# Dt's sixteen fp32 products bound behind the first sum of squares in a hybrid streaming encoder layer

## The chip, the cores and the metric

The kernel runs on one core of a Trainium2 chip (trn2). The metric is device time in microseconds (us). Before the change three runs gave 1318.94, 1319.08 and 1319.94 us, so the median is 1319.08 us. Besides these there is one profiled execution, from which all rows come. The engines are named as the profile names them: PE (matmuls), PEld (PE's weight loads), DVE, ACT, POOL, and SP, which issues most DMAs.

## The reference, cut to what matters

One inference step of one layer for 256 prompt rows and 32 sample rows (NT = 288 together), model width 2048:

```
xn   = rmsnorm(x, norm_mix_pre)
proj = xn @ w_in                   # [u_pool 1024 | z 2048 | xBC 2560 | dt 32]
pool = trailing means of u_pool, projected
ssd  = chunked scan: conv and silu of xBC; dt = softplus(dt_raw + bias); gate silu(z); grouped rmsnorm
x    = x + rmsnorm(concat[pool, ssd] @ w_out)
x    = x + rmsnorm(ConvFFN(rmsnorm(x)))      # w_up 2048 -> 11264, conv, silu gate, w_down
```

The change concerns the 32 columns of dt alone. All of the layer's other work is computed by the same instructions before and after.

## The kernel before, in words

Activations lie transposed, channels on 128 partitions and the 288 rows along the free axis. Each of the large products is done in three matmuls (`mm3`, lines 135 to 137): weights and activations are split into a high part in fp32r and a low rest, and hi·hi, hi·lo and lo·hi are summed in PSUM. The split of a weight tile is one ACT instruction (`whi`, line 129; line 283 in the first projection) and one DVE instruction (`wlo`, line 130; line 284). Four buffers each hold `raw` (the weights as loaded), `whi` and `wlo`. The rows after this call the three matmuls of a step *main matmuls*; a weight tile of 1024 columns feeds 24 of them.

The instructions are written in program order, and a scheduler puts them into a fixed order for each engine when the kernel is built. Every engine then runs its own list strictly in order. `tc.issue_after(ins)` binds what is written under it behind an instruction, `tc.keep_in_program_order` fixes a matmul's place on PE, and `tc.high_priority` draws an instruction forward.

The first projection (written out at lines 255 to 295) treats six 128-column blocks of xBC: the four of B and C and the first two of x. Its loop over k (16 tiles of 128 input channels) loads `xT` and `raw`, makes `xn` (line 98 on ACT and 99 on DVE), splits the weights, and issues 18 main matmuls per k into six PSUM sums `first` (five `acc`, one `acc_x`). Meanwhile ACT squares the input tiles and POOL adds them into `xsum` (line 233). At k = 14, ahead of that tile's 18 main matmuls, `input_rstd` multiplies `xsum` by a matrix of 1/2048 (`prs`, line 241, one fp32 matmul, recorded as two), ACT takes the root (line 236) and DVE the reciprocal (line 237): that is `rstd`.

Dt has too few columns for that scheme. Its weights (`wdt`, 128 x 16 x 32) are scaled by norm_mix_pre on DVE (line 299), and 16 fp32 products of 32 columns each (`pdt`, line 304, recorded as 32) go into four quarters of one PSUM tile, so that four partial sums stand on the partitions. DVE multiplies them by `rstd` (`v4`, line 306, `v` in the profile's rows), and one more fp32 matmul with `sel4` (`pv`, line 308) adds the four quarters. From `pv` comes dt's chain on 32 partitions: softplus by a series (`ser`), the running sum `r`, the table `g` (lines 401 to 405), which SP stores to DRAM (`g_d`, line 407) and loads again spread over all partitions (`gb`, line 453, 0.8 MB for each group of four heads).

`ssd_four` uses `gb`: ACT makes `ce`, `elast` and the decay mask `m` from it (lines 460 to 474), DVE multiplies `m` by the products of B and C (line 476), and PE multiplies it with the scaled x (`py`, lines 483 to 489). Eight such groups are spread over the projections of x and z. PSUM has five `acc` banks and three banks of a second pool, which `acc_x`, `prs`, `pdt`, `pv`, `py` and the like share in turn. Sums of the first projection leave PSUM through DVE (`conv_in`, lines 341 and 342, into `ebuf`), multiplied by `rstd`.

`xT` and `wdt` lie in a memory pool that is closed behind `pv`; the mixer's tiles take its place (`aneg`, line 391, `scan_one`, line 321, `h0t`, line 455), so their first writers wait for the end of `pdt`.

## Time and profile before

| what | value |
| --- | --- |
| runs, median | 1319.08 us (1318.94 to 1319.94) |
| the profiled execution's own time | 1318.3 us |
| its span, first to last instruction | 1316.4 us |
| granted PE clock | 1.000 |
| PE busy | 1310.2 us of the span |
| DVE, ACT, POOL busy | 895.7, 671.6, 229.7 us |
| first projection with prs and pdt on PE | 5.07 to 46 us |
| projections of x and z with the scan | 46 to about 282 us |

A row of the timeline gives the start in us, the duration in us, the engine, the line, the operation with output and inputs, sizes and a count; square brackets show idle time ahead of it and what ended it. Matmuls overlap in the records (a row of 0.29 us starts 0.13 us behind the one ahead), so the cost of a matmul is the distance between starts. A row of the windows gives, for a stretch of the span, how long each engine was busy in it. A row of the waits gives an engine and line, what it waited for, the total in us, how often, and the longest.

### The profile page before, as it was taken

What the parts mean: (1) busy time and instruction counts of PE and PEld (TensorE: products, weight loads), DVE (VectorE), ACT (ScalarE), POOL (GpSimd) and SP (SyncE); (2) the same over time, 40 slices, a digit from 0 to 9 for tenths busy, and PEclk for the clock granted to TensorE, in tenths of its full rate; (3) what the DMA queues carried; (4) which work ended last, traced back from release to release, by engine and by line L of the source; (5) the groups of instructions that cost most, each with busy time, mean ns of one, the idle gap of its engine ahead of it and who ended that gap; (6) DMA issues with size and microseconds to landing.
All of it is one profiled execution on the core that took longest, in us unless ns stands there. A gap on an engine that the chain in (4) does not pass through costs nothing.

```text
span 1316.4 us, 25204 instructions
## 1 busy us (share of the span) xinstructions
PE 1310.2 (100%) x10067; PEld 1298.4 (99%) x10067; DVE 895.7 (68%) x1486; ACT 671.6 (51%) x1010; POOL 229.7 (17%) x363
## 2 busy tenths in 40 slices
PE   9999999999999999999999999999999999999998
PEld 9999999999999999999999999999999999999997
DVE  8889988679654599977766744336666666664544
ACT  7558866446543466554444433334444454444443
POOL 6321221211430200211211200001111111101110
PEclk9999999999999999999999999999999999999999
DMA  9668874465665556666444445445445554466663
GB/s 350 186 209 279 278 223 145 165 221 204 208 219 181 183 167 213 187 184 203 168 161 165 160 168 173 158 171 185 168 161 165 180 169 161 163 235 187 203 179 109
DMA packets 104996, 249.81 MB, mean 190 GB/s; under 512 B 64272, under 2 KB 70352, under 8 KB 82608
## 3 DMA queue, kind: packets, MB, share of 16 engines
q1 hardware_dynamic: 102784, 243.44, 56.3%
q0 software_dynamic: 1664, 4.59, 1.2%
q8 instruction: 78, 1.28, 0.4%
q14 instruction: 38, 0.31, 0.1%
q10 hardware_dynamic: 432, 0.19, 0.1%
HBM read 236.23 MB, written 11.95 MB: 189 GB/s over the span
## 4 chain that ended last, share of the span: by engine, by line
PE 100%; ACT 0%; issue 0%; POOL 0%; DVE 0%; POOLq 0%
PE acc L135 31%; PE acc L137 31%; PE acc L136 31%; PE acc_x L137 1%; PE acc_x L135 1%; PE acc_x L136 1%; PE py L483 1%; PE pst L780 0%; PE run_a L1121 0%; PE low L1119 0%; PE idle L249 0%; PE run_b L1134 0%; PE py L485 0%; PE pdt L304 0%; PE py L489 0%; PE py L487 0%
## 5 line engine op out<-in xcount | busy, mean ns | idle before, releaser
L130 DVE TENSOR_TENSOR wlo<-raw,whi 128x1024 fp32r<-128x1024 f32 (+1 forms) x386 | 463.4, 1202 | 321.1 <-ACT whi L129 318.5
L129 ACT ACTIVATE whi<-raw 128x1024 fp32r<-128x1024 f32 (+1 forms) x386 | 400.1, 1037 | 476.8 <-PE acc L136 375.1
L135 PE MATMUL acc<-hn,whi 128*128 128x288 f32 x1360 | 393.3, 294 | 0.0
L136 PE MATMUL acc<-hn,whi 128*128 128x288 f32 x1360 | 392.7, 293 | 0.0
L137 PE MATMUL acc<-hn,wlo 128*128 128x288 f32 x1360 | 391.9, 293 | 0.0
L135 PEld LDWEIGHTS acc<-hn,whi 128*128 128x128 f32 x1360 | 253.3, 188 | 0.4 <-ACT hn L880 0.4
L136 PEld LDWEIGHTS acc<-hn,whi 128*128 128x128 f32 x1360 | 253.4, 188 | 0.1
L137 PEld LDWEIGHTS acc<-hn,wlo 128*128 128x128 f32 x1360 | 253.3, 188 | 0.0
L135 PE MATMUL acc<-xn,whi 128*128 128x288 f32 x688 | 203.2, 296 | 0.0
L136 PE MATMUL acc<-xn,whi 128*128 128x288 f32 x688 | 201.0, 293 | 0.0
L137 PE MATMUL acc<-xn,wlo 128*128 128x288 f32 x688 | 199.6, 295 | 0.0
L135 PE MATMUL acc<-fa,whi 128*128 128x288 f32 x660 | 194.0, 294 | 0.0
L136 PE MATMUL acc<-fa,whi 128*128 128x288 f32 x660 | 193.4, 293 | 0.0
L137 PE MATMUL acc<-fa,wlo 128*128 128x288 f32 x660 | 193.1, 293 | 0.0
L135 PEld LDWEIGHTS acc<-xn,whi 128*128 128x128 f32 x688 | 129.4, 188 | 1.3 <-issue 0.9
L136 PEld LDWEIGHTS acc<-xn,whi 128*128 128x128 f32 x688 | 129.2, 188 | 0.4
L137 PEld LDWEIGHTS acc<-xn,wlo 128*128 128x128 f32 x688 | 128.1, 188 | 0.0
L135 PEld LDWEIGHTS acc<-fa,whi 128*128 128x128 f32 x660 | 124.1, 188 | 0.0
L136 PEld LDWEIGHTS acc<-fa,whi 128*128 128x128 f32 x660 | 123.9, 188 | 0.0
L137 PEld LDWEIGHTS acc<-fa,wlo 128*128 128x128 f32 x660 | 123.9, 188 | 0.0
L932 POOL COPY fc_stage<-ebuf 128x4 f32<-128x4 f32 x88 | 28.4, 323 | 523.3 <-DVE ebuf L931 523.3
L928 POOL COPY ebuf<-pf 128x2 f32<-128x2 f32 x88 | 72.4, 824 | 122.2 <-DVE fc L938 70.2
(307 smaller groups left out, 1741.9 us busy)
## 6 DMA issues: line engine op xcount, KB each, us to landing
raw<-in_w_up SPq DMA_DIRECT2D x80, 1024.0 KB, 4.8
raw<-in_w_in SPq DMA_DIRECT2D x38, 1024.0 KB, 5.2
raw<-in_w_down SPq DMA_DIRECT2D x32, 1024.0 KB, 4.8
raw<-in_w_out SPq DMA_DIRECT2D x23, 1024.0 KB, 4.8
raw<-in_w_down SPq DMA_DIRECT2D x16, 768.0 KB, 4.2
raw<-in_w_up SPq DMA_DIRECT2D x8, 896.0 KB, 4.6
gb<-g_d SPq DMA_DIRECT2D x8, 832.0 KB, 6.6
raw<-in_w_first SPq DMA_DIRECT2D x5, 768.0 KB, 7.3
```

What stands on the lines that cost most here:

```text
L129: act.activation(hi, raw[:, k : k + n, :], AF.Copy)
L130: dve.tensor_tensor(lo, raw[:, k : k + n, :], hi.bitcast(F32), op=ALU.subtract)
L135: pe.matmul(out, wh, a[:, 0, :], start=start, stop=False)
L136: pe.matmul(out, wh, a[:, 1, :], start=False, stop=False)
L137: pe.matmul(out, wl, a[:, 0, :], start=False, stop=stop)
L483: pe.matmul(y[:, 0:256], xw[:, 0, c], m[:, j, 0:256], start=True, stop=False)
L928: pool.tensor_copy(e[:, 258:260], pf[:, 4:6, i])
L932: pool.tensor_copy(fc_stage[:, :, :, i], e[:, 256:324].rearrange("p (s c) -> p s c", c=34)[:, :, 0:2])
```

## The change

Three things are written at other places; no instruction is added or taken away.

- The sum that makes `sel4` from the identity is written ahead of the first projection.
- The scaling of `wdt` on DVE is bound behind the split of the thirteenth weight tile (k = 12).
- The 16 products `pdt` are written directly behind `input_rstd()` at k = 14 and kept in program order, so ahead of the 36 main matmuls of k = 14 and 15. Their PSUM tile is requested ahead of the loop.

```diff
     first = [acc_ps.tile([P, NT], F32, tag="acc", name="acc") if m < 5 else aux([P, NT], "acc_x") for m in range(6)]
     chunks = ((0, 1), (1, 1)) + tuple((k, 2) for k in range(2, KD, 2))
+    sel4 = const.tile([P, HEADS], F32, name="sel4")
+    dve.tensor_reduce(sel4, ident.rearrange("p (q h) -> p h q", h=HEADS), axis=AX.X, op=ALU.add)
+    p_dt = aux([P, NT], "pdt")
...
             cut.append((w_hi, w_lo))
+            if k == 12:
+                with tc.issue_after(w_lo.ins):
+                    dve.tensor_tensor(
+                        wdt, wdt, g_mix_pre.unsqueeze(2).broadcast_to([P, KD, HEADS]), op=ALU.mult
+                    )
...
             if k == 14:
                 input_rstd()
+                for r in range(4):
+                    for q in range(4):
+                        i = 4 * q + r
+                        o = p_dt[HEADS * q : HEADS * (q + 1), :]
+                        tc.keep_in_program_order(
+                            pe.matmul(o, wdt[:, i, :], xT[:, i, :], start=r == 0, stop=r == 3)
+                        )
             for m in range(6):
                 c = slice(m * P, (m + 1) * P)
                 mm3(first[m], hi[:, c], lo[:, c], a, k == 0, k == KD - 1)
 
-    sel4 = const.tile([P, HEADS], F32, name="sel4")
-    dve.tensor_reduce(sel4, ident.rearrange("p (q h) -> p h q", h=HEADS), axis=AX.X, op=ALU.add)
-    dve.tensor_tensor(wdt, wdt, g_mix_pre.unsqueeze(2).broadcast_to([P, KD, HEADS]), op=ALU.mult)
-    p_ = aux([P, NT], "pdt")
-    for r in range(4):
-        for q in range(4):
-            k = 4 * q + r
-            pe.matmul(p_[HEADS * q : HEADS * (q + 1), :], wdt[:, k, :], xT[:, k, :], start=r == 0, stop=r == 3)
     v4 = const.tile([P, NT], F32, tag="spread", bufs=3, name="v4")
-    dve.tensor_tensor(v4, p_, rstd, op=ALU.mult)
+    dve.tensor_tensor(v4, p_dt, rstd, op=ALU.mult)
     first_dt = aux([HEADS, NT], "pv")
     pe.matmul(first_dt, sel4, v4, start=True, stop=True)
```

Since a scheduler makes the order, the move goes further than these lines. Three places show it; the rows are those of the built programs. In the changed kernel line numbers behind the edit are larger by eight.

On PE, at k = 14 of the first projection, the piece of the difference is this (lines that are only renumbered left aside):

```order
 L137 MATMUL acc_x<-xn,wlo 128x288
 L241 MATMUL prs<-xsum,mean 128x288
+L306 MATMUL pdt<-xT,wdt 32x288 x16
 L135 MATMUL acc<-xn,whi 128x288
 L136 MATMUL acc<-xn,whi 128x288
```

The 16 products now stand between `prs` and the first main matmul of k = 14. Where they stood before, behind the last main matmul of k = 15, the changed kernel has `pv`:

```order
L135 MATMUL acc_x<-xn,whi 128x288
L136 MATMUL acc_x<-xn,whi 128x288
L137 MATMUL acc_x<-xn,wlo 128x288
L316 MATMUL pv<-v_658,sel_151 32x288
L135 MATMUL acc<-xn,whi 128x288
```

Before, 30 main matmuls of the second projection stood between `pdt` and `pv`. Up to here both kernels now have run the same work on PE, in another order.

On DVE, around the reciprocal that makes `rstd` (`ebuf_111` to `ebuf_117` take the first four sums out of PSUM, `v_658` is v4), before:

```order
L130 TENSOR_TENSOR wlo<-raw,whi 128x1024 x2
L237 RECIPROCAL rstd<-rstd 128x288
L130 TENSOR_TENSOR wlo<-raw,whi 128x1024
L341 TENSOR_TENSOR ebuf_111<-acc,rstd 128x256
L341 TENSOR_TENSOR ebuf_113<-acc,rstd 128x256
L342 TENSOR_TENSOR ebuf_111<-acc,rstd 128x32
L341 TENSOR_TENSOR ebuf_115<-acc,rstd 128x256
L342 TENSOR_TENSOR ebuf_113<-acc,rstd 128x32
L341 TENSOR_TENSOR ebuf_117<-acc,rstd 128x256
L342 TENSOR_TENSOR ebuf_115<-acc,rstd 128x32
L342 TENSOR_TENSOR ebuf_117<-acc,rstd 128x32
L130 TENSOR_TENSOR wlo<-raw,whi 128x1024
```

and in the changed kernel:

```order
L130 TENSOR_TENSOR wlo<-raw,whi 128x1024 x2
L237 RECIPROCAL rstd<-rstd 128x288
L314 TENSOR_TENSOR v_658<-pdt,rstd 128x288
L349 TENSOR_TENSOR ebuf_111<-acc,rstd 128x256
L350 TENSOR_TENSOR ebuf_111<-acc,rstd 128x32
L349 TENSOR_TENSOR ebuf_113<-acc,rstd 128x256
L350 TENSOR_TENSOR ebuf_113<-acc,rstd 128x32
L130 TENSOR_TENSOR wlo<-raw,whi 128x1024
```

v4 comes directly behind the reciprocal, where it was behind two weight splits and eight evictions; the third weight split of the second projection comes behind two evicted sums. Further on, dt's chain on DVE stands one weight split further ahead: the last part of `g` behind the 17th split of the w_in weights, not the 18th, and the first product of `m` behind the 22nd, not the 23rd. The first `py` on PE has 815 main matmuls ahead of it, not 833.

On SP's DMA queue, where `g` goes out and comes back, before:

```order
L174 DMA xs_d<-blocks 32x9x32 x4
L457 DMA xw<-xs_d 128x2x256
L458 DMA xw<-xs_d 128x256
L114 DMA raw<-in_w_in 128x2048
L174 DMA xs_d<-blocks 32x9x32 x4
L114 DMA raw<-in_w_in 128x2048
L407 DMA g_d<-g 32x416
L174 DMA xs_d<-blocks 32x9x32 x4
L453 DMA gb<-g_d 128x1664 x2
```

and in the changed kernel:

```order
L174 DMA xs_d<-blocks 32x9x32 x4
L415 DMA g_d<-g 32x416
L465 DMA xw<-xs_d 128x2x256
L466 DMA xw<-xs_d 128x256
L461 DMA gb<-g_d 128x1664
L114 DMA raw<-in_w_in 128x2048
L174 DMA xs_d<-blocks 32x9x32 x4
L461 DMA gb<-g_d 128x1664
```

The store of `g` has moved ahead of two weight loads and one store of x, and the first load of `gb` ahead of two of each; the second `gb` stands behind one weight load and one store. Behind the point that lies at 225 us in the trace of before, all engines have the same rows with the same waits in both kernels.

## The prediction

> **What bounds the kernel now.** I read the page first: the span, each engine's busy time and the chain that ended last.

> ```profile
> span 1316.4 us, 25204 instructions
> PE 1310.2 (100%) x10067; PEld 1298.4 (99%) x10067; DVE 895.7 (68%) x1486; ACT 671.6 (51%) x1010; POOL 229.7 (17%) x363
> PE 100%; ACT 0%; issue 0%; POOL 0%; DVE 0%; POOLq 0%
> ```

> PE is busy throughout, and the chain runs over PE alone. A busy PE can still be a slow one, so I looked at the stretch in which the two orders differ, 51 to 290 us, in the windows, and then at PE's waits and PE's weight loads' waits over the whole span.

> ```profile
> 51.00:290.00 239.00, 239.00 (x1940) 233.74 (x1939) 207.74 (x386) 150.41 (x272) 53.73 (x62) 1.00 0.67 213
> ```
> ```profile
> PE idle L249 <- POOL mean L182: 1.2, 1, 1.2
> PE y_ps L1164 <- ACT diag L1163: 0.6, 1, 0.6
> ```
> ```profile
> PEld py L483 <- issue: 0.8, 5, 0.2
> PEld py L483 <- PE acc L136: 0.7, 4, 0.2
> ```

> PE is busy for all 239.00 us at a granted clock of 1.00. It waits by name twice: at the very start and near the end, neither of them in a stretch that changes. The largest waits of its weight loads at the changed places are 0.8 and 0.7 us in all. So the time of this kernel is the sum of PE's matmuls, and a change of order is worth only what it saves in passages from one kind of matmul to another, or costs in a wait that isn't there now. What a main matmul costs, and what the fp32 groups cost, shows in the timeline of PE:

> ```profile
> 36.19 0.29 PE L135 MATMUL acc<-xn,whi 128*128 128x288 f32 x1
> ...
> 38.41 0.29 PE L137 MATMUL acc_x<-xn,wlo 128*128 128x288 f32 x1
> 38.55 0.65 PE L241 MATMUL prs<-xsum,mean 128*128 128x288 f32 x2
> 38.81 0.51 PE L135 MATMUL acc<-xn,whi 128*128 128x288 f32 x1
> 39.16 0.29 PE L136 MATMUL acc<-xn,whi 128*128 128x288 f32 x1
> ...
> 43.63 0.29 PE L137 MATMUL acc_x<-xn,wlo 128*128 128x288 f32 x1
> 43.85 2.15 PE L304 MATMUL pdt<-xT,wdt 128*32 128x288 f32 x32
> 45.93 0.40 PE L135 MATMUL acc<-xn,whi 128*128 128x288 f32 x1
> 46.17 0.29 PE L136 MATMUL acc<-xn,whi 128*128 128x288 f32 x1
> ...
> 49.85 0.29 PE L137 MATMUL acc<-xn,wlo 128*128 128x288 f32 x1
> 50.07 0.67 PE L308 MATMUL pv<-v,sel 128*32 128x288 f32 x2
> 50.67 0.40 PE L135 MATMUL acc<-xn,whi 128*128 128x288 f32 x1
> 50.91 0.29 PE L136 MATMUL acc<-xn,whi 128*128 128x288 f32 x1
> ```

> From 36.19 to 38.55 there are 18 main matmuls, so one costs 0.131 us. A group's whole cost is the distance from the main matmul ahead of it to the second behind it, less two of these (0.26): `prs` 39.16 - 38.41 - 0.26 = 0.49 us, `pdt` 46.17 - 43.63 - 0.26 = 2.28, `pv` 50.91 - 49.85 - 0.26 = 0.80.

> **The change part by part.** *The products moved behind `prs`.* Nothing is added: the same 16 products, 36 main matmuls later before, directly behind `prs` now. `prs` and `pdt` become one group with one passage to main matmuls fewer. That passage is bounded from both sides. Behind `prs` the first main matmul starts 0.26 us in and the next 0.35 later, 0.22 more than the usual 0.13; ahead of `pdt` the gap is 43.85 - 43.63 - 0.13 = 0.09. If both vanish, 0.31 us are saved; the other end is that a product of another kind pays the same as a main matmul. Before has one place where a full-size fp32 matmul stands directly beside a group of narrow ones, `psum_g` behind `py`, and the same group of `py` without it:

> ```profile
> 212.17 0.29 PE L137 MATMUL acc<-xn,wlo 128*128 128x288 f32 x1
> 212.39 1.08 PE L483 MATMUL py<-m,xw 128*64 128x256 f32 x8
> ...
> 214.28 0.75 PE L496 MATMUL psum_g<-gsum,mean 128*128 128x288 f32 x2
> ...
> 215.00 0.29 PE L136 MATMUL acc<-xn,whi 128*128 128x288 f32 x1
> ```
> ```profile
> 227.32 0.29 PE L137 MATMUL acc<-xn,wlo 128*128 128x288 f32 x1
> ...
> 229.67 0.29 PE L136 MATMUL acc<-xn,whi 128*128 128x288 f32 x1
> ```

> Together they cost 215.00 - 212.17 - 0.26 = 2.57 us, `py` alone 229.67 - 227.32 - 0.26 = 2.09: `psum_g` adds 0.48, as much as `prs` costs by itself. Joining saved 0.01. That is the nearest row, so I take a saving of 0.05 us and keep 0 to 0.31 for the range.

> The rows ahead of and behind a narrow group show a gap of 0.09 and one of 0.11 us. [...]

> *The scaling of `wdt`.* It is one DVE instruction of 1.30 us, at 23.48 us before, and goes behind the split of k = 12:

> ```profile
> 23.48 1.30 DVE L299 TENSOR_TENSOR wdt<-wdt,g 128x512 f32<-128x512 f32 x1
> ```

> It must end before `pdt` starts at about 39 us, and the split of k = 12 ends near 31, so it ends near 32.3. The splits behind it come 1.3 us less early than they would, but the work ahead of it has become 1.3 us shorter, so they end when they did. Cost: nothing. `sel4` was at the head of DVE's list already.

> *`pv` moved from behind 30 main matmuls to behind the last of k = 15.* Its turn is 46.1 us: the main matmul at 43.63, `pdt`'s 2.28, one pitch of 0.13 and the gap of 0.09, less the 0.05. What it waits for is v4:

> ```profile
> 39.69 1.28 ACT L236 ACT_TABLE_LOAD   x1
> 40.98 0.50 ACT L236 ACTIVATE rstd<-prs,eps_t 128x288 f32<-128x288 f32 x1
> 41.52 1.95 DVE L237 RECIPROCAL rstd<-rstd 128x288 f32<-128x288 f32 x1 [0.58 <-ACT rstd L236]
> ...
> 47.31 0.45 DVE L306 TENSOR_TENSOR v<-pdt,rstd 128x288 f32<-128x288 f32 x1
> ```

> The root and the reciprocal stand where they did, behind the same work, so the reciprocal ends at 43.47. v4 now follows directly and ends at 43.9, while `pdt` itself is done at about 41. So `pv` has 2.2 us in hand and costs its 0.80 as before. Behind `pv` stands the whole second projection. Its first sum needs the bank of `first`'s first block, whose last matmul ends near 44.3; the two evictions, about 0.5 us, end at 44.8, and the bank is wanted at 46.7.

> *What this makes earlier.* `pdt`'s end releases its pool 5 us earlier for the mixer's tiles, and ACT loads the Exp table and makes `aneg` 1.5 us ahead of the third weight split. That split must wait for PE to leave a buffer at about 43.5 in any case, and `aneg` is done at 43.0. Dt's chain on DVE moves one weight split forward, which is 24 x 0.131 = 3.15 us. The consumers on PE move too: the first `py` by 18 main matmuls, 2.4 us. Their margins are in the rows of the scan:

> ```profile
> 95.12 0.32 SPq L407 DMA_DIRECT2D g_d<-g  x1
> ...
> 101.32 0.81 SPq L453 DMA_DIRECT2D gb<-g_d  x2
> ```
> ```profile
> 105.96 0.31 ACT L460 ACTIVATE ce<-gb 128x128 f32<-128x128 f32 x1 [1.78 <-DMA gb<-g_d]
> ```
> ```profile
> 117.97 1.88 DVE L476 TENSOR_TENSOR m<-m,cbt 128x1664 f32<-128x1664 f32 x1
> ```
> ```profile
> 122.00 1.08 PE L483 MATMUL py<-m,xw 128*64 128x256 f32 x8
> ```

> Before, `gb` landed at 105.96, the first masked `m` ended 13.9 us later at 119.85, and `py` began at 122.00: 2.15 us in hand. After, `gb` should land one split earlier, at 102.8, `m` should end at 116.7, and `py`'s turn is 122.00 - 2.36 = 119.6: 2.9 us in hand. No wait appears and none goes, since there was none.

> **Sum.** The profiled execution took 1318.3 us, of which 1316.4 are the span. The change takes 0.05 us off the span. The median of the runs lies 0.78 above the profiled execution, so 1319.08 - 0.05 = **1319.0 us**.

> **The rivals.** *`pv` becomes a wait.* If v4 comes as late as before, at 47.76, PE stands still from 46.1 for 1.7 us: 1320.7 us. Against it: v4 directly behind the reciprocal in DVE's list. For it: `pv` now has no main matmuls of the second projection ahead of it to cover a delay, and the turn comes 4 us earlier.

> *PE waits for the first `py`, slower.* `gb` now stands in SP's queue behind the second store of x, and the second `gb` behind a weight load and the third store. SP waits at both kinds of places:

> ```profile
> SPq L114 <- DVE wlo L130: 98.0, 23, 13.7
> SPq L174 <- DVE blocks L171: 29.0, 12, 6.4
> ```

> If the store ahead of `g_d` waits for its transposed block the longest time seen, 6.4 us, `gb` lands at 109.2, `m` ends at 123.1 and PE stands 3.5 us: 1322.5 us. The deciding point is a landing at 105.7; beyond 108.4 the loss exceeds the bound of 0.2%. With a weight load's longest wait, 13.7, it would be 10.8 us and 1329.8. For it: ACT waited 1.78 us for this very load before, and the weight splits queue behind it on ACT. Against it: the scheduler's order has kept over 2 us in hand here, and the longest waits are those of a queue that runs ahead of its buffers.

> *The waits of the narrow groups go, faster.* With dt's chain earlier, the two rows of `py`'s weight loads (0.8 and 0.7 us) could vanish, and the 0.31 of the joined group with them: 1319.08 - 1.8 = 1317.3 us. Against it: nine waits of at most 0.2 us look like the passage that each group pays, and the groups remain. That the change doesn't do what it says is excluded by the order: the products do stand behind `prs`.

> **How the numbers follow.** About 0.2% (2.6 us) is what a measurement of this kernel can tell from no change. The forecast has 0.84, `pv`'s wait 0.05, the late `gb` 0.07, and the vanished waits 0.04. The first two are within the bound; the third is beyond it; of the fourth I count half beyond, should its price be too low. So faster 0.02, same 0.91, slower 0.07. The range takes the profiled execution's 1318.3 less the whole 0.31, 1318.0, and at the top the highest run, 1319.94, with half a microsecond for a small wait, 1320.5. It leaves out most of the two slower cases and part of the faster one, together less than 2 in 10.

> **What would show it.** Right: PE's row in the window from 51 to 290 us still full; `prs` and `pdt` in one group of 2.5 to 2.8 us; the reciprocal ending near 43.5 and v4 near 43.9; `pv` starting near 46.1 behind a gap of 0.1; `py` near 119.6 and the masked `m` about 3 us ahead of it. Wrong: a row of PE waiting for DVE's v4, for `m` or for a weight split, above all between 105 and 150 us; or a span more than 0.5 us shorter, which would mean that the passages cost more than the rows of `psum_g` say.

## The result and the profile after

The changed kernel takes 1327.74 us (median of six runs, 1325.79 to 1332.05), the kernel before 1319.01 us in the same series (1318.46 to 1319.94): a ratio of 1.0067, with a 95% interval of 1.0058 to 1.0077. The change makes the kernel 8.7 us slower, where 1319.0 us was predicted. The profiled execution took 1327.84 us, its span is 9.5 us longer than that of before. From the page of after: the span, the engines' busy times, and the chain that ended last.

```profile
span 1325.9 us, 25212 instructions
PE 1313.5 (99%) x10067; PEld 1300.3 (98%) x10067; DVE 896.7 (68%) x1486; ACT 670.3 (51%) x1010; POOL 222.2 (17%) x363
PE 94%; DMA 2%; DVE 2%; SPq 1%; issue 1%; ACT 0%; DVEq 0%; POOL 0%; POOLq 0%
```

The chain no longer runs over PE alone: DMA and DVE have come in. The window that was full before (239.00 us of PE) is the next view, and then PE's waits by name within it.

```profile
51.00:290.00 239.00, 232.82 (x1870) 226.43 (x1869) 200.28 (x363) 146.01 (x268) 44.40 (x58) 0.99 0.66 210
```
```profile
PE acc L137 <- DVE wlo L130: 5.8, 3, 2.6
PE acc L135 <- ACT whi L129: 0.4, 1, 0.4
```

PE stands for 6.2 us, nearly all for the low part of a weight split, which is DVE's work. The clock's mean is 0.99 instead of 1.00, and that counts as well, as the timeline of PE at the stalls shows (line numbers behind the edit are larger by eight):

```profile
173.18 0.29 PE L136 MATMUL acc<-xn,whi 128*128 128x288 f32 x1
176.06 0.41 PE L137 MATMUL acc<-xn,wlo 128*128 128x288 f32 x1 [2.59 <-DVE wlo L130]
176.29 0.41 PE L135 MATMUL acc<-xn,whi 128*128 128x288 f32 x1
...
179.81 0.30 PE L135 MATMUL acc<-xn,whi 128*128 128x288 f32 x1
...
205.61 0.29 PE L136 MATMUL acc<-xn,whi 128*128 128x288 f32 x1
208.33 0.40 PE L137 MATMUL acc<-xn,wlo 128*128 128x288 f32 x1 [2.43 <-DVE wlo L130]
```

Between 173.18 and 179.81 us stand 17 steps of one main matmul, which cost 2.23 us at 0.131 each and took 6.63 here: 2.75 us are the wait, 1.65 are 16 matmuls at a distance of 0.24 us, that is at half the clock (0.50 granted). A second group of waits, at 204 to 213 us, costs 4.4 us (by the main matmuls' starts against those of before). The two together make 8.8 of the 9.5 us; by 213 us all of the loss has arrived.

Whom DVE waited for in the stretch from 40 to 290 us, at the two lines that handle x; in the changed kernel

```profile
DVE blocks L171 <- DMA xs_d<-blocks: 13.0, 6, 4.1
DVE xw L474 <- DMA xw<-xs_d: 3.5, 4, 1.6
```

and before:

```profile
DVE blocks L171 <- DMA xs_d<-blocks: 4.2, 4, 2.5
DVE xw L466 <- DMA xw<-xs_d: 3.6, 3, 1.3
```

Each of x's sixteen tiles, when its convolution is done, is transposed in blocks on DVE (line 171) into the tile `blocks`, of which there is **one buffer**; SP stores it by four DMAs (line 174) into `xs_d`, in pieces of 128 bytes, and `ssd_four` loads x from there as `xw`. The next transposition must wait until those four stores have landed, and DVE's list is in order, so a weight split behind it waits too. These two waits together I call **the x waits**: 7.8 us before, 16.5 after. The first stall, seen from DVE in the changed kernel:

```profile
164.72 0.47 DVE L171 STREAM_TRANSPOSE blocks<-xs 128x288 f32<-128x288 f32 x1
...
173.35 0.48 DVE L171 STREAM_TRANSPOSE blocks<-xs 128x288 f32<-128x288 f32 x1 [2.72 <-DMA xs_d<-blocks]
...
174.78 1.22 DVE L130 TENSOR_TENSOR wlo<-raw,whi 128x1024 fp32r<-128x1024 f32 x1
```

The block written from 164.72 us on was stored late enough to hold DVE for 2.72 us at 173.35; the split behind it ends at 176.00, and PE goes on at 176.06. Without that wait the split would have ended 2.7 us earlier, at 173.3, just when PE wanted it. At the second stall there is no wait for a DMA: DVE's last waits for x, of 3.10 and 0.70 us, end at 190.00 and 195.16 us, from then on it works without a gap through what has piled up, and the split of 207.06 us comes 7.8 us behind the one before it.

What the prediction had worked out is there as well. PE's timeline at the moved products, at `pv` and at the first `py`:

```profile
38.69 0.29 PE L137 MATMUL acc_x<-xn,wlo 128*128 128x288 f32 x1
38.82 0.65 PE L241 MATMUL prs<-xsum,mean 128*128 128x288 f32 x2
39.40 2.15 PE L306 MATMUL pdt<-xT,wdt 128*32 128x288 f32 x32
41.48 0.40 PE L135 MATMUL acc<-xn,whi 128*128 128x288 f32 x1
41.72 0.29 PE L136 MATMUL acc<-xn,whi 128*128 128x288 f32 x1
...
46.17 0.29 PE L137 MATMUL acc_x<-xn,wlo 128*128 128x288 f32 x1
46.40 0.67 PE L316 MATMUL pv<-v,sel 128*32 128x288 f32 x2
...
119.92 1.08 PE L491 MATMUL py<-m,xw 128*64 128x256 f32 x8
```

No wait stands at any of the three places.

### The profile page after: what moved, and what is told of

It is laid out like the page before. It is cut to its first block, busy times and chain, and to the rows that moved or that the text cites. A ratio compares the mean times of both kernels' runs of the same rounds, so it can differ in the third digit from the quotient of the medians.

```text
span 1325.9 us, 25212 instructions
## 1 busy us (share of the span) xinstructions
PE 1313.5 (99%) x10067; PEld 1300.3 (98%) x10067; DVE 896.7 (68%) x1486; ACT 670.3 (51%) x1010; POOL 222.2 (17%) x363
## 3 DMA queue, kind: packets, MB, share of 16 engines
q8 instruction: 78, 1.28, 0.4%
## 4 chain that ended last, share of the span: by engine, by line
PE 94%; DMA 2%; DVE 2%; SPq 1%; issue 1%; ACT 0%; DVEq 0%; POOL 0%; POOLq 0%
PE acc L137 30%; PE acc L135 29%; PE acc L136 29%; DMA xs_d<-blocks 2%; SPq L174 1%; PE acc_x L137 1%; PE acc_x L135 1%; PE acc_x L136 1%; DVE wlo L130 0%; PE pst L788 0%; PE py L491 0%; PE run_a L1129 0%; PE low L1127 0%; PE idle L249 0%; PE run_b L1142 0%
## 5 line engine op out<-in xcount | busy, mean ns | idle before, releaser
L130 DVE TENSOR_TENSOR wlo<-raw,whi 128x1024 fp32r<-128x1024 f32 (+1 forms) x386 | 463.9, 1203 | 314.2 <-ACT whi L129 311.9
L135 PE MATMUL acc<-hn,whi 128*128 128x288 f32 x1360 | 393.3, 294 | 0.0
L136 PE MATMUL acc<-hn,whi 128*128 128x288 f32 x1360 | 392.7, 293 | 0.0
L137 PE MATMUL acc<-hn,wlo 128*128 128x288 f32 x1360 | 391.9, 293 | 0.0
L135 PEld LDWEIGHTS acc<-hn,whi 128*128 128x128 f32 x1360 | 253.3, 188 | 0.4 <-ACT hn L888 0.4
L136 PEld LDWEIGHTS acc<-hn,whi 128*128 128x128 f32 x1360 | 253.3, 188 | 0.1
L137 PEld LDWEIGHTS acc<-hn,wlo 128*128 128x128 f32 x1360 | 253.3, 188 | 0.0
L137 PE MATMUL acc<-xn,wlo 128*128 128x288 f32 x688 | 202.5, 299 | 5.8 <-DVE wlo L130 5.8
L135 PE MATMUL acc<-xn,whi 128*128 128x288 f32 x688 | 203.6, 297 | 0.4 <-ACT whi L129 0.4
L136 PE MATMUL acc<-xn,whi 128*128 128x288 f32 x688 | 200.7, 293 | 0.0
L135 PE MATMUL acc<-fa,whi 128*128 128x288 f32 x660 | 194.0, 294 | 0.0
L136 PE MATMUL acc<-fa,whi 128*128 128x288 f32 x660 | 193.4, 293 | 0.0
L137 PE MATMUL acc<-fa,wlo 128*128 128x288 f32 x660 | 193.1, 293 | 0.0
L137 PEld LDWEIGHTS acc<-xn,wlo 128*128 128x128 f32 x688 | 128.9, 189 | 6.8 <-DVE wlo L130 6.6
L135 PEld LDWEIGHTS acc<-xn,whi 128*128 128x128 f32 x688 | 130.0, 189 | 2.1 <-ACT whi L129 0.7
L136 PEld LDWEIGHTS acc<-xn,whi 128*128 128x128 f32 x688 | 129.9, 189 | 0.2
L135 PEld LDWEIGHTS acc<-fa,whi 128*128 128x128 f32 x660 | 124.1, 188 | 0.0
L137 PEld LDWEIGHTS acc<-fa,wlo 128*128 128x128 f32 x660 | 123.9, 188 | 0.0
L136 PEld LDWEIGHTS acc<-fa,whi 128*128 128x128 f32 x660 | 123.9, 188 | 0.0
```

The lines of the kernel that those rows point to most:

```text
L130: dve.tensor_tensor(lo, raw[:, k : k + n, :], hi.bitcast(F32), op=ALU.subtract)
L135: pe.matmul(out, wh, a[:, 0, :], start=start, stop=False)
L136: pe.matmul(out, wh, a[:, 1, :], start=False, stop=False)
L137: pe.matmul(out, wl, a[:, 0, :], start=False, stop=stop)
```

## Where x's blocks became late

The third and the fifth transposition of the mixer are those of x tiles 0 and 2. On DVE's timeline, before:

```profile
77.48 0.47 DVE L171 STREAM_TRANSPOSE blocks<-xs 128x288 f32<-128x288 f32 x1
...
90.06 0.47 DVE L171 STREAM_TRANSPOSE blocks<-xs 128x288 f32<-128x288 f32 x1
```

and in the changed kernel:

```profile
82.12 0.46 DVE L171 STREAM_TRANSPOSE blocks<-xs 128x288 f32<-128x288 f32 x1
...
94.06 0.46 DVE L171 STREAM_TRANSPOSE blocks<-xs 128x288 f32<-128x288 f32 x1
```

They start 4.6 and 4.0 us later. x tile 2's stores landed at 97.5 us before and at 105.4 in the changed kernel (the semaphores' times in the traces); the last transposition starts at 190.6 and at 201.4. So the delay of 4 us has grown to 11; ahead of the first stall, at x tile 9 (146.9 and 157.4 us), it was 10.5 already. Where the first 4 us come from shows on ACT, which makes the tanh of each convolution; before:

```profile
51.32 0.88 ACT L358 ACTIVATE tanh<-conv 128x291 f32<-128x291 f32 x2 [0.69 <-DVE conv L354]
...
53.21 1.07 ACT L129 ACTIVATE whi<-raw 128x1024 fp32r<-128x1024 f32 x1
```

and in the changed kernel:

```profile
50.37 1.06 ACT L129 ACTIVATE whi<-raw 128x1024 fp32r<-128x1024 f32 x1 [2.88 <-PE acc L136]
...
53.46 1.06 ACT L129 ACTIVATE whi<-raw 128x1024 fp32r<-128x1024 f32 x1 [1.23 <-PE acc L136]
54.43 0.77 ACT L366 ACTIVATE tanh<-conv 128x291 f32<-128x291 f32 x2
```

In the new order one split more stands ahead of the tanh, and a split waits there until PE has left a buffer. One split is 24 of PE's main matmuls, 3.15 us. Counted in the built lists (splits of the later projections ahead of each pair's tanh on ACT, and the store of x behind which the first two loads of `gb` stand in SP's queue):

| tanh of | before | changed | e9 | e15 | e16 |
| --- | --- | --- | --- | --- | --- |
| B/C tiles 0, 1 | 5 | 6 | 5 | 5 | 6 |
| B/C tiles 2, 3 | 9 | 10 | 9 | 8 and 9 | 10 |
| x tiles 0, 1 | 12 and 13 | 14 | 12 and 13 | 12 | 13 and 14 |
| x tiles 2, 3 | 16 | 17 and 18 | 16 | 15 and 16 | 16 and 18 |
| gb's first two loads behind x tile | 3 | 1 and 2 | 2 | 4 | 2 |

With the products early, `pdt`'s bank and the memory under `aneg` come free earlier, and the scheduler made other lists for all engines (that it did so for this reason is argued, not shown). The experiments ask which part of that carries the time.

## The experiments

Medians are of all runs of a kernel, with the lowest and highest; the kernel before had medians of 1318.89 to 1319.33 us beside them. The theories in the expectations: **S**, late stores of x hold DVE at the one buffer, so that splits come late; **O**, the new order alone puts too much of DVE's work ahead of the splits; **T** and **G**, worked out later, name the late tanh and the early `gb` as what makes the stores late; **D** names dt's early chain.

One caution holds for nearly all of them: an edit gives the scheduler something else to order, so it moves rows on other engines as well. e1 differs from the changed kernel, and e2 from before, by little more than the one instruction. But DVE's list in e3 and e11 differs from the changed kernel's from 60 and 88 us on, and in e7 from that of before from 82 us on. Whether a run differs by its waits or by the work in its list is therefore asked once more behind the table of all runs.

### Each part alone

e1 is the changed kernel without the binding of `wdt`'s scaling (the diff), e2 the kernel before with the bound scaling at k = 12 alone:

```diff
-                with tc.issue_after(w_lo.ins):
-                    dve.tensor_tensor(
-                        wdt, wdt, g_mix_pre.unsqueeze(2).broadcast_to([P, KD, HEADS]), op=ALU.mult
-                    )
+                dve.tensor_tensor(
+                    wdt, wdt, g_mix_pre.unsqueeze(2).broadcast_to([P, KD, HEADS]), op=ALU.mult
+                )
```

> The changed kernel without the binding of dt's weight scaling: only the sixteen products (and sel4) are moved; the scaling is left where the scheduler puts it. The built order equals the changed kernel's on all engines but for that one DVE instruction. Theory S (stores: the earlier dt chain pushes the transposed x stores behind the loads of gb; DVE waits for the one transpose buffer, weight splits come late, PE stands near 173 and 206 us) expects the whole loss, 1326 to 1329 us. The rival that the binding of the scaling holds DVE up in the first projection expects 1319.

> The kernel before with the scaling of dt's weights bound behind the thirteenth tile's split and nothing else. The built order equals that of before but for this DVE instruction. Theory S expects no change, 1318.5 to 1320 us. The rival that the binding is to blame expects 1326 to 1329.

e1: 1327.9 us (1326.98 to 1331.21), ratio 1.0073 (1.0055 to 1.009). e2: 1319.03 us (1318.31 to 1320.59), ratio 1.0003 (0.9994 to 1.0012). The products' move, with the lists that the scheduler makes of it, carries the whole loss; the scaling is free, as predicted.

### A second transpose buffer

e3 is the changed kernel and e4 the kernel before with

```diff
...
-        s = pool_.tile([P, NT], F32, tag="blocks", bufs=1, name="blocks")
+        s = pool_.tile([P, NT], F32, tag="blocks", bufs=2 if two else 1, name="blocks")
...
```

for the blocks of the mixer.

> The changed kernel with two buffers for the transposed blocks in the mixer instead of one. Theory S expects DVE's wait for the stores (13.0 us between 40 and 290 us in the changed kernel) to fall under 3 us, no PE wait over 0.5 us between 51 and 290 us, and 1318.5 to 1320 us. Rival O (the new order alone has too much DVE work ahead of the weight splits, whatever the buffers) expects PE to wait for weight splits still, by 4 us or more, and 1324 us or more.

> The kernel before with two buffers for the transposed blocks. Control for the run with the changed kernel: PE is full already, so both theories expect 1318.5 to 1320 us, with DVE's wait for the stores falling from 4.2 us to under 2.

e3: 1319.89 us (1318.4 to 1323.02), ratio 1.0008 (0.9999 to 1.0017). e4: 1320.87 us (1319.38 to 1322.46), ratio 1.0015 (1.0006 to 1.0024). In e3 no wait of PE is left in the stretch, and DVE's list of waits has none for `blocks`:

```profile
DVE xw L474 <- DMA xw<-xs_d: 6.6, 5, 3.1
```

The first blocks are as late as in the changed kernel (x tile 0 at 82.1 us), yet the loss is gone: late blocks cost nothing here, where DVE need not wait for the buffer. e4 lies above what was expected: there the x waits have moved to the loads, 13.5 us of `xw` with 5.3 at once, and PE stands 2.3 us for splits. Two buffers are no cure in themselves.

### dt's chain held back

e5 keeps the products early and binds `v4` behind the last eviction of the first sums, so that `pv` is back at its old place on PE.

```diff
...
+    bc_in = [conv_in(NX + i, first[i]) for i in range(4)]
     v4 = const.tile([P, NT], F32, tag="spread", bufs=3, name="v4")
-    dve.tensor_tensor(v4, p_dt, rstd, op=ALU.mult)
+    with tc.issue_after(gone[0].ins):
+        dve.tensor_tensor(v4, p_dt, rstd, op=ALU.mult)
...
```

> The changed kernel with the products still early, but v4 bound behind the last of the first projection's evictions, so that pv stands at row 307 of PE's list (304 before, 275 changed) and dt's scan at row 128 of DVE's (133 before, 123 changed); the third to sixth transposed blocks of DVE then stand at rows 110, 123, 141 and 155 (before 105, 115, 132, 146; changed 111, 125, 141, 166). Theory S: the time is set by how late the stores of transposed x land, whichever step made them late; with dt's chain half way back the waits of DVE for the one transpose buffer lie between 4.2 and 13.0 us in the stretch from 40 to 290 us, and the time between 1319 and 1325 us, by the waits of PE for a weight split that are left (0 to 5 us). If it were the products' new place on PE itself, pv's place would not matter: 1327 to 1328 us with 6 us of PE's waits. Rival O: dt's chain half way back leaves half of the loss, 1323 us, with the waits for the buffer unchanged at about 13 us.

1330.75 us (1330.11 to 1330.97), ratio 1.0089 (1.0074 to 1.0104): slower still, and outside every theory's range. Its waits on DVE and PE:

```profile
DVE xw L476 <- DMA xw<-xs_d: 10.3, 6, 4.2
DVE blocks L171 <- DMA xs_d<-blocks: 10.2, 7, 3.3
```
```profile
PE acc L137 <- DVE wlo L130: 7.6, 4, 3.3
```

With 20.5 us it has the most of the x waits of all runs, and x tile 0 starts at 83.3 us though dt's chain stands half way back. So holding dt's chain back does not bring the blocks forward, as S had it at first; in e5 the tanh of B/C stand behind six splits, as in the changed kernel. That gave theory T.

### gb on another queue

e6 issues `gb`'s loads from POOL:

```diff
-        sp.dma_start(out=gb, in_=g_d[4 * q : 4 * q + 4, :].unsqueeze(0).broadcast_to([P, 4, MW]))
+        pool.dma_start(out=gb, in_=g_d[4 * q : 4 * q + 4, :].unsqueeze(0).broadcast_to([P, 4, MW]))
```

> The changed kernel with the loads of gb issued by GpSimd's queue instead of SyncE's; PE's order differs from the changed kernel's in 4 rows and DVE's in some 20. Theory S, as put before these runs, makes the loads of gb ahead of the third stores a part of the lateness (4 of its 8 to 11 us): if the packets of gb still go to the same 16 engines, the stores land only a little earlier, and the time is 1323 to 1328 us; if the place in SyncE's queue is what delays the stores, DVE's waits for the buffer fall from 13.0 to below 9 us and the time to 1319 to 1323 us. Rival O: the order on DVE is the same, so 1327 to 1329 us with PE's waits at 173 and 206 us as they are.

1328.08 us (1324.82 to 1330.23), ratio 1.0067 (1.0051 to 1.0083). x tile 2's stores landed 13.5 us behind their transposition, 11.3 in the changed kernel. Taking `gb` out of SP's queue did not bring the stores forward. S had them land a little earlier in this case. The time is just above S's 1323 to 1328 us and within O's 1327 to 1329, so it hardly tells them apart.

### Stores written twice, without the change

e7 is the kernel before, in which each block of x is stored a second time into a tensor that nobody reads:

```diff
+        if again is not None:
+            av = again[:, t * P : (t + 1) * P].rearrange("(j r) (i f) -> i r j f", r=32, f=32)
+            for i in range(4):
+                sp.dma_start(out=av[i], in_=s[32 * i : 32 * (i + 1), :].rearrange("r (j f) -> r j f", f=32))
...
```

> The kernel before, in which each transposed block of x is stored a second time, into a tensor that nobody reads, so that the one transpose buffer is freed later; products and dt's chain are where they were. Theory S: DVE waits for the buffer longer than the 4.2 us of before (10 to 20 us), the weight splits come late, and PE stands for wlo by 4 to 12 us, at half clock behind the longer waits: 1324 to 1335 us. Rival O: the order of DVE's work is that of before, so PE doesn't wait: 1319 to 1320.5 us.

1327.27 us (1326.88 to 1329.97), ratio 1.0067 (1.0052 to 1.0082). DVE's waits (the second store is named `xs`), then PE's:

```profile
DVE blocks L171 <- DMA xs<-blocks: 9.2, 5, 3.9
DVE xw L470 <- DMA xw<-xs_d: 7.4, 5, 3.3
```
```profile
PE acc L137 <- DVE wlo L130: 4.1, 4, 2.1
```

The loss appears with products and dt's chain where they were, once the buffer is freed late. S's range for the time held, and its 4 to 12 us of PE's waits too (5.3); the 9.2 us at the buffer are just under its 10 to 20. O expected no wait of PE and missed by 7 us. But since DVE's list is not that of before, this run alone does not part the waits from the work.

### Splits preferred, run twice

e8, and e12 once more, is the changed kernel with

```diff
-    ahead[0] = 200
+    ahead[0] = 600
```

> The changed kernel with the weight fetches and splits of the later projections given a higher priority in the scheduler's list (600 instead of 200); PE's order is that of the changed kernel row by row, and DVE's transposes stand within 3 rows of it up to the fifteenth. Theory S: the buffer's waits stay at 10 to 14 us, since the chain of the transposes is as late as in the changed kernel, but splits stand ahead of some waiting transposes: PE's waits fall, not to nothing, 1320 to 1326 us. Rival O: the work ahead of the splits is what counts; with the splits first PE doesn't wait, 1319 to 1320 us, though DVE's waits for the buffer are as long.

> One more look at the kernel with the splits preferred, whose five runs lay at 1319.2 and at 1324.7 to 1326.5 us with the same order of instructions; the profile there was of the shortest, with 2.8 us of DVE's waits for the buffer and no wait of PE. Theories S and T: a run of 1325 us shows longer landings of the stores, DVE's waits of 8 us or more and PE standing for wlo near 175 or 205 us, 4 to 7 us with the half clock behind. If something outside this chain made the difference, the waits for the buffer are at 3 us in a long run too.

e8: 1325.32 us (1319.2 to 1326.49, five runs), ratio 1.0051 (1.0035 to 1.0068); e12, one run: 1324.36 us. The lists are the same in both, the times are not. The profile of e8 fell on the run of 1319.2 us, with no wait of PE in the stretch; its DVE:

```profile
DVE xw L474 <- DMA xw<-xs_d: 4.8, 5, 2.4
DVE blocks L171 <- DMA xs_d<-blocks: 2.8, 6, 1.0
```

The profile of e12, of the run of 1324.36 us:

```profile
DVE xw L474 <- DMA xw<-xs_d: 8.5, 5, 3.4
DVE blocks L171 <- DMA xs_d<-blocks: 3.5, 3, 2.7
```

For e8, S had expected 10 to 14 us at the buffer and O as long waits without a loss; there were 2.8. For a long run I had expected 8 us or more; it is 3.5 in e12, and the rest is in the loads of `xw`. The sum, 7.6 against 12.0 us, goes with the time. PE stood 2.4 us in e12, and half clock followed (0.51 from 204.20 to 207.60 us). So the same order gives both times, and what differs in the two traces is how the transfers of x land: the kernel stands at an edge. (e12 ran on another chip; e8's own five runs hold both times.)

### tanh put back

e9 binds five splits on ACT behind the tanh that stood ahead of them before; e10 a sixth one (`21: 9`).

```diff
+    n_split, tanhs, split_behind = [0], [], {6: 1, 10: 3, 13: 4, 14: 5, 17: 7}
...
+                n_split[0] += 1
+                if n_split[0] in split_behind:
+                    order.enter_context(tc.issue_after(tanhs[split_behind[n_split[0]]].ins))
...
-        act.activation(th, c, AF.Tanh)
+        tanhs.append(act.activation(th, c, AF.Tanh))
```

> The changed kernel with five weight splits of ACT bound behind the tanh that stood ahead of them before (the 6th behind the second B/C tile's, the 10th behind the fourth's, the 13th, 14th and 17th behind those of x tiles 0, 1 and 3); products and dt's chain stay early. In ACT's list the pairs of tanh then stand behind 5, 9, 12 to 13 and 16 splits of the second projection, as before (changed: 6, 10, 14, 17 to 18). Theory T, formed after the run with dt held: the stores are late because ACT does these tanh one split (3.15 us) later, where it waits for PE; put back, the third transposed block starts near 78 to 80 us instead of 82.1, the last near 191 to 196 instead of 201.4, PE stands for wlo by less than 2 us, and the time is 1319 to 1322 us. Rival D: dt's chain, which is still early, is what delays the blocks on DVE: no change, 1325 to 1329 us.

> As the run before, with a sixth binding (the 21st split behind x tile 5's tanh), which gives another order behind 120 us. Theory T: 1319 to 1322 us again, by the same early blocks, whatever the order behind. Rival D: 1325 to 1329 us.

e9: 1325.62 us (1322.36 to 1327.27), ratio 1.0044 (1.003 to 1.0059). e10: 1323.01 us (1319.89 to 1326.77), ratio 1.003 (1.0017 to 1.0043). The head of the chain is back, as T said: x tile 0's block starts at 79.0 and 78.4 us, tile 2's at 91.3 and 90.7. But the last one starts at 199.2 and 200.3, near the changed kernel's 201.4: x tile 6's block, at 129.0 and 129.7, is as late as in the changed kernel (129.0; before 120.1). T's 1319 to 1322 us was missed by both; e9 lies in D's range of 1325 to 1329, e10 between the two. So T explains the first 4 us and at most part of the loss, and D, which expected no change, is wrong for e10. Nor was the late tanh wholly undone: counted in the built lists, x tile 6's stands behind 25 splits in e9 and 26 in e10, behind 23 in the kernel before and in the changed one.

### Stores packed

e11 writes each block contiguously, 1152 bytes a row instead of nine pieces of 128, and loads it so. x thereby reaches the scan in another order, and what depends on it is not the reference's.

```diff
...
-        dv = d[:, t * P : (t + 1) * P].rearrange("(j r) (i f) -> i r j f", r=32, f=32)
-            sp.dma_start(out=dv[i], in_=s[32 * i : 32 * (i + 1), :].rearrange("r (j f) -> r j f", f=32))
+            at = P * NT * t + 32 * NT * i
+            sp.dma_start(
+                out=d.rearrange("n c -> (n c)")[at : at + 32 * NT].rearrange("(r f) -> r f", f=NT),
+                in_=s[32 * i : 32 * (i + 1), :],
+            )
...
```

> The changed kernel with the transposed blocks of x written contiguously, 1152 bytes a row instead of nine pieces of 128 bytes, and read back by loads of the same size; x thereby reaches the scan in another order, so the outputs that depend on it are not the reference's. The tanh stay late. If the landing of the stores behind the one buffer carries the loss (theories S and T alike), stores land within 2 to 3 us, DVE's waits for the buffer fall below 4 us, and the time is 1319 to 1321 us though every block starts as late as in the changed kernel. If lateness alone cost the time, 1325 to 1329 us.

1319.27 us (1318.19 to 1320.02), ratio 1.0 (0.9991 to 1.0009); no wait of PE in the stretch.

```profile
DVE xw L486 <- DMA xw<-xs_d: 4.5, 3, 1.9
DVE blocks L179 <- DMA xs_d<-blocks: 3.4, 5, 1.4
```

The median store lands in 3.9 us (4.6 in the changed kernel; I had expected 2 to 3), and DVE's waits for the buffer are 3.4 us: the blocks start as late as in the changed kernel up to x tile 2 (93.6 us), the last one at 189.7, before the kernel before's 190.6. So the chain catches up. How much of this is the size of the pieces and how much the other lists of e11 is not shown.

### gb put back, both put back, part of the products put back

e13 binds `gb`'s first loads behind the stores of x tiles 3, 3, 4 and 5, as before; e14 has this and e9's bindings; e15 and e16 leave the last 8, or the last 4, of the 16 products in the old place.

```diff
+            if q < 4:
+                order.enter_context(tc.issue_after(x_out[(3, 3, 4, 5)[q]].ins))
...
```
```diff
-                for r in range(4):
+                for r in range(2):
...
+    for r in range(2, 4):
+        for q in range(4):
+            i = 4 * q + r
+            pe.matmul(p_dt[HEADS * q : HEADS * (q + 1), :], wdt[:, i, :], xT[:, i, :], start=False, stop=r == 3)
```

> The changed kernel with the first loads of gb bound in SyncE's queue where they stood before: the first two behind x tile 3's stores (changed: ahead of tile 2's and tile 3's), the third behind tile 4's, the fourth behind tile 5's. tanh stays one split late. Theory G (gb's 832 KB ahead of the stores make them land late): tile 2's stores land within 8 us of their transposition (changed 11.3, before 7.4), DVE's waits for x's stores and loads (blocks and xw) fall from 16.5 us to 8 to 12, and the time to 1319.5 to 1322.5 us. Theory T (the late tanh): 1325 to 1329 us, since every block starts as late as in the changed kernel.

> Both bindings together: gb behind x tile 3's stores, and five splits behind the tanh that stood ahead of them before. The products are early, but ACT's tanh and SyncE's gb stand as before. If T and G together are the cause, DVE's waits for x's stores and loads are 6 to 10 us (before 7.8), PE stands less than 1 us for a split, and the time is 1319 to 1321 us. If the cause is elsewhere (dt's chain early, which is not undone), 1323 to 1328 us.

> The changed kernel with only the first 8 of dt's 16 products behind the sum of squares and the other 8 in the old place, 36 main matmuls later. That gives one more group of fp32 products on PE, 0.2 to 0.6 us by the rows of the groups. In ACT's list the pairs of tanh stand behind 5, 8 to 9, 12 and 15 to 16 splits (before 5, 9, 12 to 13, 16), and gb's first loads behind x tile 4's stores. Theories T and G: 1319 to 1321.5 us, with 6 to 10 us of DVE's waits for x's stores and loads. If early products by themselves cost the time, half of the loss stays: 1323 to 1325 us.

> The changed kernel with 12 of dt's 16 products behind the sum of squares and 4 in the old place. tanh stands behind 6, 10, 13 to 14 and 16 to 18 splits, that is as late as in the changed kernel, but gb's first loads stand behind x tile 3's stores, as before. Theory T: 1324 to 1329 us, with over 12 us of DVE's waits for x's stores and loads. Theory G: 1319 to 1322 us, with less than 12. By the relation of the runs so far (up to 8 us of these waits no loss, 12 us 1 to 5 us, 16 and more 8 to 12 us) the waits and the time must agree in either case.

e13: 1323.6 us (1323.33 to 1326.05), ratio 1.0038 (1.0023 to 1.0053). e14: 1322.68 us (1318.12 to 1326.75, ten runs), ratio 1.0018 (1.0005 to 1.0031). e15: 1319.39 us (1318.36 to 1320.71), ratio 1.0001 (0.9991 to 1.0011). e16: 1326.43 us (1325.74 to 1328.34), ratio 1.0058 (1.0043 to 1.0073).

In e13 x tile 2's stores still landed 10.1 us behind the transposition, and the x waits were 15.0 us: G had said 8 us and 8 to 12, so `gb` is not the cause by itself, though half of the loss is gone; the time lies between G's range and T's. e14 should have had 6 to 10 us of x waits by T and G together, and had 16.0; its time, too, lies between the two ranges. In e16 `gb`'s loads stand behind x tile 2's stores, not tile 3's as its expectation says, so it holds nothing against G; by T it came as expected. e15 is the one kernel with early products, one buffer and the stores as they are that loses nothing. Its x waits:

```profile
DVE blocks L171 <- DMA xs_d<-blocks: 5.8, 5, 3.3
DVE xw L478 <- DMA xw<-xs_d: 2.1, 4, 1.0
```

### All runs by the x waits

For each profiled execution: the x waits of DVE, and PE's waits for DVE and ACT, both from 40 to 290 us (0.9 us of e5's, all of e15's and 4.2 us of e16's are waits at `py` that the view puts to issue; e16's stands where DVE had waited 4.47 us for `xw`), and the execution's own time.

| kernel | x waits, us | PE's waits, us | own time, us |
| --- | --- | --- | --- |
| e3, two buffers | 6.6 | 0 | 1318.4 |
| e8, splits preferred | 7.6 | 0 | 1319.2 |
| before | 7.8 | 0 | 1318.3 |
| e11, packed | 7.9 | 0 | 1318.97 |
| e15, half early | 7.9 | 0.5 | 1319.73 |
| e2, scaling only | 9.3 | 0 | 1318.93 |
| e12, as e8 | 12.0 | 2.4 | 1324.36 |
| e10, tanh back | 12.3 | 0.5 | 1320.62 |
| e4, before with two buffers | 13.5 | 2.3 | 1322.46 |
| e13, gb back | 15.0 | 3.3 | 1323.86 |
| e14, both back | 16.0 | 2.0 | 1323.25 |
| changed | 16.5 | 6.2 | 1327.84 |
| e7, stores twice | 16.6 | 5.3 | 1327.34 |
| e16, twelve early | 16.6 | 6.7 | 1328.34 |
| e6, gb on POOL | 17.0 | 6.0 | 1330.23 |
| e1, products only | 17.1 | 5.4 | 1328.68 |
| e9, tanh back | 17.6 | 4.5 | 1326.92 |
| e5, dt held | 20.5 | 8.5 | 1330.97 |

Up to 9.3 us of x waits cost nothing; from 12 us on PE waits, and the own time follows, though not step by step (16.0 us in e14 cost less than 12.0 in e12): it counts where a wait falls. The prediction's window row fits this: DVE was busy for 207.74 of the 239 us before, so, by an estimate from that row, some 31 us were free for all that it waits for.

Is it these waits that make the splits late, or more work ahead of them (O)? The first stall ends with the 37th split of the w_in weights on DVE. It starts at 164.55 us before, at 174.78 in the changed kernel and at 173.86 in e7. The windows from the start of the span up to it, in this order:

```profile
0.00:164.55 164.55, 163.34 (x1295) 158.24 (x1296) 150.02 (x281) 117.12 (x225) 56.38 (x97) 1.00 0.79 260
0.00:174.78 174.78, 172.26 (x1357) 166.41 (x1357) 150.26 (x280) 118.03 (x226) 49.56 (x97) 1.00 0.76 249
0.00:173.86 173.86, 170.61 (x1347) 165.46 (x1348) 149.22 (x279) 118.61 (x228) 47.12 (x97) 1.00 0.77 249
```

DVE's busy time, the third one, is the same within 1.1 us: ahead of this split DVE has as much work in all three, and it comes 9 to 10 us later by waits alone. In e3 and e11, which lose nothing, it starts at 166.83 and 165.72 us behind 149.52 and 150.42 us of work. At the second stall (the 45th split, at 194.82 us before and 207.06 in the changed kernel) 1.2 us of the 12.2 are more work. So O is out for the first stall, and has at most a small part in the second. Of the waits that make up the 10.2 us, the x waits are the larger part: up to the 37th split they are 4.8 us before and 11.4 in the changed kernel; the rest is longer waits for ACT and PE.

**What is shown:** the loss comes from weight splits that are late on DVE, and they are late by waits, of which those for the transfers of x are the larger part. With these waits taken away in two ways the loss is gone (e3, e11), with them put in without the change it is there (e7), and the same lists take 1319.2 us with 7.6 us of them and 1324.36 with 12.0 (e8, e12). The products' place on PE is not it (all sixteen are early in e3 and e11, eight in e15, and these lose nothing), nor is the scaling (e2). **What stays open:** which of the many moved instructions makes the stores late. With the tanh put back (e9, e10) or `gb` (e13) the median is 2 to 5 us lower, but both put back still lose 3.4 us at the median (e14), with runs from 1318 to 1327, and each binding also moved instructions elsewhere.

## Why the prediction was wrong, point by point

- **What bounds the kernel**: right. The time is PE's matmuls plus waits that are not there before, and the whole loss is waits and what follows them.
- **The joined group**: right. `prs` with `pdt` cost 41.72 - 38.69 - 0.26 = 2.77 us, as much as both apart (0.49 + 2.28); the joining saved nothing, against 0.05 taken and 0 to 0.31 as bounds.
- **The scaling of `wdt`**: right, e2.
- **`pv`**: right. It starts at 46.40 us (46.1 predicted) behind a gap of 0.10, and `v4` was no wait.
- **What this makes earlier**: right that the first `py` has no wait; it starts at 119.92 us (119.6 predicted). But the margin was smaller than worked out: the masked `m` ends at 118.72 us, 1.2 us ahead of `py` and not 2.9, since DVE had waited 1.57 us for `xw` just ahead of it.
- **"No wait appears and none goes, since there was none"**: this is the step that failed. It checked the margins of dt's own consumers and stopped at 120 us. What had to give way to dt's earlier chain was not followed: the convolutions' tanh on ACT and the blocks of x on DVE, 4 us later at tile 0 and 11 at the last. And what covers PE was not looked at: the weight splits, in the list of an engine with 31 us to spare in 239 and with waits for transfers in it. DVE's waits were never read; the row of 4.2 us at `blocks` would have shown a buffer without a spare. Among its signs of being wrong the prediction does name PE waiting for a weight split, but between 105 and 150 us; the waits came at 173 to 176 and at 205 to 213.
- **The rivals**: the second one, a wait through SP's queue, came nearest. It named stores of x that stand for their blocks, but priced the late `gb` at the first `py` (1322.5 us, up to 1329.8). `gb` came in time; what was late were the stores themselves, whom DVE and then the splits wait for. Its sizes, 3.5 to 10.8 us, would have held the result, but by luck, since the wait that they price did not occur; it had a chance of 0.07, and the range left it out.
- **A size that no step had**: the half clock behind a wait, 1.65 of the first stall's 4.4 us.

## What to carry to other kernels

Where a scheduler makes the order, a move of a few instructions is a new order for every engine: compare all lists to the end of the stretch, and ask for each engine what now stands behind what, not only whether the moved work's own consumers are in time. An engine that feeds the bound one must be read by its slack (busy time, plus its waits for transfers, against the stretch), and a single buffer between an in-order engine and a store is a wait as long as the stores take to land (DVE's waits at `blocks`: 4.2 us in all before, 13.0 in the changed kernel). If runs of one kernel scatter by more than those of its neighbours (1318 to 1327 us in e14), it stands at such an edge.

## What the runs showed of the hardware

**A wait may cost more than itself, or not, by where it falls.** In the changed kernel the granted clock is 0.50 for 3.413 us, from 176.31 us on, and the main matmuls in this stretch stand 0.24 us apart instead of 0.131. Four windows of the changed kernel, each 3.41 us long, two around the first stall and two around the second. The borders are those of the stretch at half clock, carried on in steps of 3.413 us. That the steps hold is an estimate from where stretches at half clock start: at 177.76 and 208.48 us in e1, nine such steps apart, and at 176.31 and 1323.19 us in the changed kernel, 336 steps apart. In the rows the columns are the length, then busy times of PE, PEld, DVE, ACT and POOL, the granted clock, DMA share and GB/s:

```profile
172.85:176.27 3.42, 0.83 (x6) 0.61 (x5) 2.92 (x6) 1.39 (x2) 0.00 (x0) 1.00 1.00 403
176.30:179.70 3.40, 3.40 (x16) 3.40 (x16) 3.40 (x5) 1.80 (x4) 0.00 (x0) 0.50 0.39 83
```
```profile
203.58:206.99 3.41, 1.89 (x13) 1.42 (x11) 3.38 (x6) 3.41 (x6) 2.13 (x2) 1.00 0.64 180
206.99:210.41 3.42, 2.08 (x15) 2.08 (x16) 3.42 (x3) 3.42 (x6) 2.73 (x2) 1.00 0.01 2
```

The first stall lies within one window, in which PE was busy for 0.83 us, and the whole next window runs at half clock (0.50). The second, of 2.43 us by the row of PE (2.59 for the first), lies across a border; PE was busy for 1.89 and 2.08 us in the two windows, and the clock stays at 1.00. In e12 a shorter wait, of 1.8 us, fell into one window, and half clock followed:

```profile
200.80:204.20 3.40, 1.58 (x12) 1.35 (x11) 3.40 (x3) 3.40 (x5) 2.47 (x2) 1.00 0.02 3
204.20:207.60 3.40, 3.40 (x16) 3.40 (x15) 3.40 (x3) 0.64 (x1) 0.00 (x0) 0.51 0.00 0
```

**Stores of the same size land unevenly.** A block of x is four stores of 36 KB in pieces of 128 bytes. The median of them landed in 3.8 us before and 4.6 after, but before, a block of x took from 1.2 us (x tile 6) to 8.2 us (x tile 4) from the end of its last issue to its last landing. With pieces of 1152 bytes (e11) the same bytes held DVE for 3.4 us in all, instead of 13.0 in the changed kernel, though the median landed in 3.9 us; that the size of the pieces did this by itself is not shown.
